# Short products ahead of the 256-column stages of a two-layer decoder trunk, and a low half that is issued later

## The chip, the cores and the metric

One core of one Trainium2 chip runs the whole kernel in one launch. The metric is device microseconds of one execution, the median of several runs. TensorE (PE), VectorE (DVE), ScalarE (ACT), GpSimd (POOL) and SyncE (SP) run at the same time, each with its own list of instructions in fixed order, and wait for each other by semaphores. A TensorE product shows in the trace as a weight load (PEld) and a matmul (PE).

## The reference

Two layers over a float32 input of 512 tokens by 1024 features. Each layer is a half-step SwiGLU feed-forward block (FFN), a mixer and a second half-step FFN:

```python
D_MODEL, SEQ, DEPTH, D_FF = 1024, 512, 2, 2816
def swiglu(h, w_gate, w_up, w_down):
    return (jax.nn.silu(h @ w_gate) * (h @ w_up)) @ w_down
# in each layer:
#   x += 1/2 * post(SwiGLU_1(pre(x)))
#   h = pre(x); P = h @ W_in    (HGRN2 q/f/i/out-gate, attention q/k/v, two branch gates)
#   A = HGRN2 recurrence(P) -> W_bA;  B = sliding-window attention(P) -> W_bB
#   x += post((sigmoid(gA)*A + sigmoid(gB)*B) @ W_out)
#   x += 1/2 * post(SwiGLU_2(pre(x)))
```

`pre` and `post` are RMS norms. The weights come from HBM once, as float32.

## The kernel before, in words

**Products.** TensorE works on a format that keeps part of a float32 number, so each float32 operand is split into a high half (`whi` for weights, the first `s` for activations) and a low half (`wlo`, the other `s`). One product is three matmuls, high by high, high by low and low by high (`mm3`, `wmm`). The weights lie in the array (128 rows by 128 columns) and the activations stream past, 512 tokens or a half of them, 256, at a time. All matmuls go through the helper `mm`, line L115. The order of TensorE's instructions is that in which the program's coroutines issue them; those of other engines are placed by a scheduler, except for instructions that are pinned in program order (`pin`, `hold` with `tight`).

**The weight stream.** `Stream` (`ws`) hands TensorE its weights in order, as items. Raw weights are loaded by SP into four buffers (`w32`, 128 by 1024 float32); an item's halves go into one of six pairs of tiles `whi` and `wlo`, 1024 columns in a tile of 1088, at the item's column offset `it.at`. `plain` makes items with offset 0, `pairs` makes four items a, b, c, d from two raw buffers with offset `ASIDE` = 16. Item a is the first raw buffer, b and c are sums of pieces of both (DVE, L339, L340, L346, L347), d is the last 512 columns of the second. `split` makes the halves: the high half is an ACT copy (L353). For b and c the low half is a DVE subtraction (L362). For a and d ("v" items too) ACT writes the weights with their sign turned into `wlo`, where they are cut like the high half (L357), and a DMA that POOL issues (L360) adds the raw weights to them; the low half is there when that DMA has landed. After d the two raw buffers are let go, and SP's next loads into them are issued.

**Stages.** In each FFN, `quad` comes first: four accumulators, over the first 256 tokens and then over the last 256, each half 8 steps `k` of 4 products of 256 columns (192 matmuls in both halves of a quad that has halves). There are five such quads, one in each mixer and in three of the FFNs; the first FFN has a quad without halves. The quads use the first four plain items. After some products of 512 columns come the rows of groups of seven (`fast`, `sevenths`): a row makes its gate and up products by seven products of half size in the place of eight, and takes 84 matmuls of 256 columns: 12 each for p1 and the first half of p26 (item a), 24 for both halves of p57 (item b), 24 for the second half of p26 and the first of p43 (item c), and 12 for the second half of p43 (item d). DVE puts the seven products together (L1054, L1056, L1060, L1061). The FFN of layer 0 that comes first has 15 rows, the others 19; each mixer has four such rows in its branches, each between other work. After the rows of an FFN comes `down`, with products of 512 columns, whose weights are made by DVE sums (L263), ACT (L287) and DVE (L295).

Of the kernel before, what the change touches and what calls it, by code (L numbers as in the profile page):

```python
# [7 lines left out]
F32 = mybir.dt.float32  # L8
# [3 lines left out]
ALU = mybir.AluOpType  # L12
# [3 lines left out]
P = 128  # L16
# [16 lines left out]
    first=0.0, spread=2300.0, squares=1700.0, lay=34500.0, laid=770.0, normed=7600.0, final=2600.0,  # L33
# [3 lines left out]
W32, WS, AHEAD, TAIL, FIRST, EARLY, LATE = 4, 6, 3, 4, 7, 4, 8  # L37
TURN = 0
SEVEN = 16
ASIDE = 16  # L40
ORDER = ("p1", "p3", "p7", "p2", "p6", "p5")
HEADS = (0, 4, 1, 5, 2, 6, 3, 7)

# [2 lines left out]
def trunk(ctx: ExitStack, tc: tile.TileContext, xin, wall, gains, lbT, hgain, sinks, c_dist, c_mask, c_ident, out):  # L46
    nc = tc.nc
# [99 lines left out]
    pin = tc.keep_in_program_order  # L147
# [10 lines left out]
    class Stream:  # L158
        def __init__(self):
            self.n, self.wall = 0, 0  # L160
            self.items = []
            self.raw, self.dma = {}, 0
            self.done, self.flight = 0, 0
            self.cur, self.c = 0, 0
            self.src = {}
            self.pinned = False
            self.most = AHEAD
            self.tight, self.gate = False, None
            self.side, self.freed = [], 0
            self.part = {}  # L170

        def plain(self, n, kind="u"):
            self.items += [Item(kind, self.n + i) for i in range(n)]
            for i in range(n):
                self.src.setdefault(self.n + i, self.wall + i)
            self.n += n
            self.wall += n
# [145 lines left out]
        def split(self):  # L323
            it = self.items[self.done]
            if it.kind[0] == "p":
                return self.quarter(it)
            u, last = it.u, it.kind in "uvd"
            self.load(u + (1 if it.kind in "uv" else 2))
            it.hi, it.lo = (sb.tile([P, D + 64], F32R, tag=t, name=nm(t), bufs=WS)[:, it.at : it.at + D] for t in ("whi", "wlo"))
            w, h = self.raw[u], (slice(0, D // 2), slice(D // 2, D))  # L330
            cols = (slice(0, D),)
            if it.kind == "u" and u < 2:
                cols = h
            if it.kind in "bcd":
                v = self.raw[u + 1]
            if it.kind == "b":

                self.t13 = sb.tile([P, D], F32, tag="tt", name=nm("tt"), bufs=2)
                pin(nc.vector.tensor_tensor(self.t13[:, h[0]], w[:, h[0]], v[:, h[0]], op=ALU.add))  # L339
                pin(nc.vector.tensor_tensor(self.t13[:, h[1]], v[:, h[0]], v[:, h[1]], op=ALU.add))  # L340
                w = self.t13
                self.product()
            elif it.kind == "c":

                t = sb.tile([P, D], F32, tag="tt", name=nm("tt"), bufs=2)
                pin(nc.vector.tensor_tensor(t[:, h[0]], self.t13[:, h[0]], v[:, h[1]], op=ALU.add))  # L346
                pin(nc.vector.tensor_tensor(t[:, h[1]], t[:, h[0]], w[:, h[1]], op=ALU.add))  # L347
                w = t
            elif it.kind == "d":
                w = v  # L350
                cols = h[1:]
            for c in cols:
                i = nc.scalar.copy(it.hi[:, c], w[:, c])  # L353
                if u < 6 or self.pinned or self.tight:
                    pin(i)
                if it.kind in "vad":
                    i = nc.scalar.mul(it.lo[:, c], w[:, c], -1.0)  # L357
                    if self.pinned or self.tight:
                        pin(i)
                    nc.gpsimd.dma_start(it.lo[:, c].bitcast(F32), w[:, c], accum_op=ALU.add)  # L360
                else:
                    self.hold(nc.vector.tensor_tensor(it.lo[:, c], w[:, c], it.hi[:, c].bitcast(F32), op=ALU.subtract))  # L362
            self.done += 1
            self.flight += 1
            if last:
                nu = u + (1 if it.kind in "uv" else 2)
                for i in range(u, nu):
                    self.raw.pop(i)
                    self.freed += 1
                self.load(self.freed + W32)  # L370

        def ahead(self):
            while self.done < min(len(self.items), self.cur + 1 + self.most) and self.flight < WS:
                self.split()

        def need(self, i):
            self.ahead()
            while self.done <= i:
                assert self.flight < WS
                self.split()  # L380
            return self.items[i]
# [27 lines left out]
    ws = Stream()  # L409
# [7 lines left out]
    def wmm(o, b, mv, start, stop, poll=True):  # L417

        mm3(o, b[2:], mv, start, stop)
        ws.used(b)  # L420
        if poll:
            order.poll()

    def cut(pair, c):
        return pair[0][:, c], pair[1][:, c]
# [568 lines left out]
    def quad(pre, halves):  # L994

        o = [acc() for _ in range(4)]
        blocks = {}
        ws.pinned = halves
        for half in (0, 1) if halves else (None,):
            c = WHOLE if half is None else HALF[half]  # L1000
            for k in range(KT):
                order.until(lambda: pre.have[half or 0] > k)
                for j in range(4):
                    if (k, j) not in blocks:
                        blocks[k, j] = ws.next(uses=2 if halves else 1)
                    wmm(o[j][:, c], blocks[k, j], cut(pre.h[k], c), k == 0, k == KT - 1)
            ws.pinned = False
        return o
# [17 lines left out]

    H2 = S // 2

    def sevenths(pre, between=lambda: None):

        def product(o, it, c, n):
            x = pre.operand(n)
            for k in range(4):
                wmm(o, ws.block(it, c + k), x[k], k == 0, k == 3)

        p1, p26, p57, p43 = acc()[:, :H2], acc(), acc(), aux()
        s, v = big()[:, :H2], big(F32, [P, 2, H2])
        w = ws.whole()  # L1040
        product(p1, w, 0, 1)
        ws.hold(nc.scalar.copy(s, p1))
        product(p26[:, :H2], w, 4, 2)
        between()
        w = ws.whole()
        product(p57[:, :H2], w, 0, 5)
        product(p57[:, H2:], w, 4, 7)
        c = ws.whole()
        product(p26[:, H2:], c, 0, 6)
        ws.product()  # L1050
        m = sb.tile([P, 4, H2], F32, tag="m", name=nm("m"), bufs=1)
        pairs = [p.rearrange("p (i t) -> p i t", i=2) for p in (p26, p57, p43)]

        ws.hold(nc.vector.tensor_tensor(m[:, 0:4:2, :], pairs[0], s.unsqueeze(1).to_broadcast([P, 2, H2]), op=ALU.add))  # L1054

        ws.hold(nc.vector.tensor_tensor(v, pairs[1], m[:, 2:3, :].to_broadcast([P, 2, H2]), op=ALU.add))  # L1056
        product(p43[:, :H2], c, 4, 4)
        product(p43[:, H2:], ws.whole(), 4, 3)

        ws.hold(nc.vector.tensor_tensor(m[:, 3, :], p57[:, :H2], v[:, 1, :], op=ALU.add))  # L1060
        ws.hold(nc.vector.tensor_tensor(m[:, 1:3, :], pairs[2], v[:, ::-1, :], op=ALU.add))  # L1061
        return m

    def fast(pre, a, start):
        def early():
            if j == FT - 1:
                for i in range(SEVEN, SEVEN + EARLY):
                    ws.part[i] = split(a[i])

        ws.tight = True  # L1070
        for j in range(start, FT):
            ws.most = AHEAD + (j < FT - 1)
            m = sevenths(pre, early)
            z = big(F32, [P, 2, H2])
            ws.hold(nc.scalar.activation(out=m[:, 0:2, :], in_=m[:, 0:2, :], func=AF.Silu))

            def gate(m=m, z=z):
                ws.hold(nc.vector.scalar_tensor_tensor(z, m[:, 0:2, :], -1.0, m[:, 2:4, :], op0=ALU.mult, op1=ALU.mult))

            ws.gate = gate  # L1080
            if j == FT - 1:
                ws.product()
            a.append(z.rearrange("p i t -> p (i t)"))
        ws.tight = False
# [389 lines left out]
    for l in range(DEPTH):  # L1474
        for n in (0, 2, 4):
            if n == 2:
                ws.plain(4, "v")
                ws.plain(2 * H + 2 + 8 + LATE * 3 // 2)
                for _ in range(KT - LATE // 2):
                    ws.gates()  # L1480
                ws.rows(KT, False)
            else:
                p = FIRST if l + n == 0 else 3
                ws.plain(4, "v" if l and not n else "u")
                ws.plain(min(2 * p, 8) - 4)
                ws.plain(max(2 * p - 8, 0), "v")
                ws.pairs(FT - p)
                ws.rows(FT, True)
# [154 lines left out]
```

## Time and profile before

| | |
|---|---|
| runs | 2056.76, 2056.75, 2055.87 us, median 2056.75 us |
| profiled execution | 2057.03 us, its span 2055.3 us |
| granted TensorE clock | 1.00 throughout |
| TensorE busy | 2044.0 us, 99% of the span, 13531 matmuls |
| VectorE busy | 1624.1 us, 79% |
| ScalarE busy | 1250.1 us, 61% |
| GpSimd busy | 267.6 us, 13% |
| HBM | 213.43 MB read, 14.73 MB written |

Where things are in the span: rows of the first FFN of layer 0 from 89 to 237 us, rows of its second FFN from 729 to 915 us, those of layer 1 from 1064 to 1249 us and from 1745 to 1933 us; each is followed by its `down`. The quads of the mixers and FFNs lie ahead of these stages (the first mixer's at about 349 to 372 us, the second FFN's at about 700 to 723 us). How to read the profile: busy time is the time in which an instruction of the engine was under way, and matmuls overlap, so that the share of TensorE is 99% at any distance between matmuls. The distance itself, from one matmul's start to the next one's, is read from the number of matmuls in a stretch (the xcount behind the busy time of a window, which counts also the two or three that are under way at its edge).

### The profile page before, as it was taken

The numbers are of one execution on the slowest core, as the hardware profiler recorded it, in microseconds if no ns is written. First come the engines' busy times: TensorE is split into PE (matmuls) and PEld (weight loads), VectorE is DVE, ScalarE is ACT, GpSimd is POOL, SyncE is SP. The second block draws the span as 40 slices with busy tenths as digits, with TensorE's granted clock in tenths as the row PEclk, the third lists the DMA queues.
The fourth block names the chain that finished last, engine by engine and source line by source line (L and its number), as shares of the span: only waits on it lengthen the run. The fifth ranks groups of instructions, "written<-read, shape, count | busy, mean of one in ns | idle before, by whom it ended". The sixth has DMA issues, their size and how long they took to land. (4 is left out here: it accounts for less than half of the span.)

```text
span 2055.3 us, 36503 instructions
## 1 busy us (share of the span) xinstructions
PE 2044.0 (99%) x13531; PEld 1831.3 (89%) x13531; DVE 1624.1 (79%) x2894; ACT 1250.1 (61%) x2213; POOL 267.6 (13%) x318
## 2 busy tenths in 40 slices
PE   9999999999999999999999999999999999999998
PEld 7899988877888999997899998888778989999987
DVE  5887889767676778888988788977686858788888
ACT  7556687446355556658866566864554545665684
POOL 0111140000000012113201111400000100111140
PEclk9999999999999999999999999999999999999999
DMA  8587798312247367879857778872122563788794
GB/s 256 148 188 191 175 206 239 114 64 70 73 101 207 113 151 189 189 187 208 206 151 189 192 187 207 177 232 85 62 73 62 140 193 99 181 189 195 176 199 123
DMA packets 166802, 328.07 MB, mean 160 GB/s; under 512 B 19072, under 2 KB 85088, under 8 KB 166624
## 3 DMA queue, kind: packets, MB, share of 16 engines
q1 hardware_dynamic: 122416, 228.16, 33.3%
q0 software_dynamic: 44064, 97.54, 28.2%
q8 instruction: 106, 1.74, 0.4%
q14 instruction: 72, 0.59, 0.1%
q10 hardware_dynamic: 144, 0.05, 0.0%
HBM read 213.43 MB, written 14.73 MB: 111 GB/s over the span
## 5 line engine op out<-in xcount | busy, mean ns | idle before, releaser
L115 PE MATMUL acc<-s,whi 128*128 128x256 f32 (+1 forms) x4976 | 1035.9, 306 | 0.4 <-ACT whi L353 0.4
L115 PEld LDWEIGHTS acc<-s,whi 128*128 128x128 f32 x4976 | 799.7, 189 | 47.2 <-issue 3.2
L115 PE MATMUL acc<-s,wlo 128*128 128x256 f32 (+1 forms) x2488 | 760.5, 306 | 1.0 <-DMA wlo<-w 0.8
L115 PEld LDWEIGHTS acc<-s,wlo 128*128 128x128 f32 x2488 | 468.9, 188 | 25.1 <-DMA wlo<-w 1.5
L115 PE MATMUL acc<-whi,s 128*128 128x512 f32 x1360 | 442.0, 393 | 1.4 <-DVE s L432 1.3
L353 ACT CAST whi<-w 128x1024 fp32r<-128x1024 f32 (+1 forms) x310 | 286.4, 928 | 151.0 <-PE acc L115 102.9
L353 ACT CAST whi<-tt 128x1024 fp32r<-128x1024 f32 x160 | 167.9, 1049 | 250.7 <-DVE tt L347 177.8
L360 POOL DMA_DIRECT2D wlo<-w x178 | 154.0, 867 | 1237.3 <-ACT wlo L357 532.0
L115 PEld LDWEIGHTS acc<-whi,s 128*128 128x128 f32 x1360 | 255.2, 188 | 59.6 <-issue 3.2
L362 DVE TENSOR_TENSOR wlo<-tt,whi 128x1024 fp32r<-128x1024 f32 x160 | 196.0, 1225 | 131.6 <-ACT whi L353 124.6
L115 PE MATMUL acc<-wlo,s 128*128 128x512 f32 x680 | 266.3, 392 | 1.2 <-DVE wlo L295 1.2
L115 PE MATMUL aux<-s,whi 128*128 128x256 f32 (+1 forms) x1296 | 233.1, 281 | 0.0
L362 DVE TENSOR_TENSOR wlo<-w,whi 128x1024 fp32r<-128x1024 f32 (+1 forms) x132 | 157.6, 1207 | 75.6 <-ACT whi L353 74.6
L115 PEld LDWEIGHTS aux<-s,whi 128*128 128x128 f32 x1296 | 199.1, 189 | 1.1 <-issue 0.5
L115 PE MATMUL aux<-s,wlo 128*128 128x256 f32 (+1 forms) x648 | 182.2, 281 | 0.0
L115 PEld LDWEIGHTS acc<-wlo,s 128*128 128x128 f32 x680 | 127.7, 188 | 30.0 <-DVE wlo L295 5.2
L357 ACT ACTIVATE wlo<-w 128x1024 fp32r<-128x1024 f32 (+1 forms) x178 | 153.7, 863 | 0.0
L115 PE MATMUL aux<-whi,s 128*128 128x512 f32 x432 | 143.8, 390 | 0.0
L443 POOL DMA_DIRECT2D s<-s x128 | 111.0, 969 | 218.4 <-ACT s L431 98.6
L115 PEld LDWEIGHTS aux<-s,wlo 128*128 128x128 f32 x648 | 121.9, 188 | 0.3
L295 DVE TENSOR_TENSOR wlo<-s,whi 128x512 fp32r<-128x512 f32 x160 | 103.0, 690 | 9.9 <-ACT whi L287 8.1
L431 ACT CAST s<-s 128x512 fp32r<-128x512 f32 (+1 forms) x140 | 70.8, 548 | 44.8 <-DVE s L490 39.3
(184 smaller groups left out, 2468.8 us busy)
## 6 DMA issues: line engine op xcount, KB each, us to landing
w<-wall SPq DMA_DIRECT2D x267, 512.0 KB, 4.2
wlo<-w POOLq DMA_DIRECT2D x98, 512.0 KB, 5.2
w<-wall SPq DMA_DIRECT2D x224, 128.0 KB, 3.6
wlo<-w POOLq DMA_DIRECT2D x80, 256.0 KB, 3.2
s<-wall SPq DMA_DIRECT2D x128, 128.0 KB, 4.1
s<-s POOLq DMA_DIRECT2D x64, 256.0 KB, 4.6
x_d<-s SPq DMA_DIRECT2D x48, 256.0 KB, 4.2
s<-x_d SPq DMA_DIRECT2D x48, 256.0 KB, 5.2
```

The costliest lines, as they stand in the source:

```text
L115: nc.tensor.matmul(o, lhsT, rhs, start=start, stop=stop)
L295: pin(nc.vector.tensor_tensor(it.lo[:, h[c]], w[c], it.hi[:, h[c]].bitcast(F32), op=ALU.subtract))
L353: i = nc.scalar.copy(it.hi[:, c], w[:, c])
L357: i = nc.scalar.mul(it.lo[:, c], w[:, c], -1.0)
L360: nc.gpsimd.dma_start(it.lo[:, c].bitcast(F32), w[:, c], accum_op=ALU.add)
L362: self.hold(nc.vector.tensor_tensor(it.lo[:, c], w[:, c], it.hi[:, c].bitcast(F32), op=ALU.subtract))
L431: (hold or ws.hold)(nc.scalar.copy(hi, src))
L443: nc.gpsimd.dma_start(lo.bitcast(F32), src, accum_op=ALU.add)
```

## The change

Three things are changed.

1. `lead` issues one matmul with `start` and `stop` whose result nobody reads; the next product starts its accumulator anew in the same place and overwrites it. It has 144 columns ahead of the first product of a run of rows: once ahead of each FFN's rows, and ahead of each of the 8 rows of the mixers, 12 in all. It has 112 columns ahead of the third of the 32 products of each half of each quad (step 0, accumulator 2), 10 in all. It has the same weights as the product behind it.
2. The four first items of every quad with halves get the column offset 16 in place of 0.
3. In the rows of the FFNs the low half of d is held back until the next item, which is the next row's a, is made: ACT does a high, a low and then d low, and POOL issues the DMA of a ahead of that of d. The two raw buffers of the pair are let go after d's low half, and the loads into them are issued from there. A d that is followed by another item than a is handled as before, and so are the mixers'.

```diff
+LEAD, LEAD_IN = 144, 112
...
-        def plain(self, n, kind="u"):
-            self.items += [Item(kind, self.n + i) for i in range(n)]
+        def plain(self, n, kind="u", at=0):
+            self.items += [Item(kind, self.n + i, at=at) for i in range(n)]
...
                 if it.kind in "vad":
-                    i = nc.scalar.mul(it.lo[:, c], w[:, c], -1.0)
-                    if self.pinned or self.tight:
-                        pin(i)
-                    nc.gpsimd.dma_start(it.lo[:, c].bitcast(F32), w[:, c], accum_op=ALU.add)
+                    def low(it=it, w=w, c=c):
+                        i = nc.scalar.mul(it.lo[:, c], w[:, c], -1.0)
+                        if self.pinned or self.tight:
+                            pin(i)
+                        nc.gpsimd.dma_start(it.lo[:, c].bitcast(F32), w[:, c], accum_op=ALU.add)
+                    nxt = self.items[self.done + 1].kind
+                    if it.kind == "d" and nxt == "a":
+                        self.low = low, self.done, u
+                    else:
+                        low()
+                        self.flush()
...
-            if last:
-                nu = u + (1 if it.kind in "uv" else 2)
-                for i in range(u, nu):
-                    self.raw.pop(i)
-                    self.freed += 1
-                self.load(self.freed + W32)
+            if last and not self.low:
+                self.free(u, u + (1 if it.kind in "uv" else 2))
...
+        def flush(self):
+            if self.low:
+                (low, _, u), self.low = self.low, None
+                low()
+                self.free(u, u + 2)
...
         def need(self, i):
             self.ahead()
+            if self.low and i >= self.low[1]:
+                self.flush()
...
+                    if halves and (k, j) == (0, 2):
+                        lead(o[j][:, c], blocks[k, j][2], pre.h[k][0][:, c], LEAD_IN)
                     wmm(o[j][:, c], blocks[k, j], cut(pre.h[k], c), k == 0, k == KT - 1)
...
+    def lead(o, st, mv, n):
+        mm(o[:, :n], st, mv[:, :n], True, True)
...
+        if first:
+            lead(p1, w.hi[:, :P], pre.operand(1)[0][0], LEAD)
         product(p1, w, 0, 1)
...
-            m = sevenths(pre, early)
+            m = sevenths(pre, early, j == start)
...
-                ws.plain(4, "v")
+                ws.plain(4, "v", ASIDE)
...
-                ws.plain(4, "v" if l and not n else "u")
+                ws.plain(4, "v" if l and not n else "u", ASIDE if l + n else 0)
```

On ACT, at the first rows of layer 0's first FFN, the halves of a d (the tile of 512 columns) and of the next row's a stood like this before:

```order
L353 CAST whi_983<-w_139_708 128x512
L357 ACTIVATE wlo_984<-w_139_708 128x512
L353 CAST whi_1019<-w_175_847 128x1024
L357 ACTIVATE wlo_1020<-w_175_847 128x1024
L1075 ACTIVATE m_1001<-m_1001 128x512
L353 CAST whi_1046<-tt_1048 128x1024
```

The same place of the changed kernel (a number behind a name is that of the buffer's use, and the code's lines are moved by some):

```order
L355 CAST whi_984<-w_139_708 128x512
L355 CAST whi_1014<-w_177_876 128x1024
L361 ACTIVATE wlo_1015<-w_177_876 128x1024
L361 ACTIVATE wlo_985<-w_139_708 128x512
L1104 ACTIVATE m_996<-m_996 128x512
L355 CAST whi_1047<-tt_1049 128x1024
```

The low half of d has moved behind both halves of a, and nothing else has moved between them; POOL's list shows the same exchange, the DMA of a's 1024 columns now ahead of that of d's 512.

On PE, where the first run of rows begins behind products of 512 columns, before:

```order
L115 MATMUL acc_880<-s_200,whi_703 128x512
L115 MATMUL acc_880<-s_199,wlo_704 128x512
L115 MATMUL acc_918<-s_598,whi_766 128x256 x2
L115 MATMUL acc_918<-s_598,wlo_767 128x256
L115 MATMUL acc_918<-s_623,whi_766 128x256 x2
```

And in the changed kernel:

```order
L116 MATMUL acc_880<-s_200,whi_703 128x512
L116 MATMUL acc_880<-s_199,wlo_704 128x512
L116 MATMUL acc_918<-s_598,whi_766 128x144
L116 MATMUL acc_918<-s_598,whi_766 128x256 x2
L116 MATMUL acc_918<-s_598,wlo_767 128x256
L116 MATMUL acc_918<-s_623,whi_766 128x256 x2
```

One matmul of 144 columns has come in; all of the others stand in the order of before. In the quads it is the same with 112 columns, here in the first mixer's:

```order
L116 MATMUL acc_4134<-s_4030,whi_3919 128x256
L116 MATMUL acc_4134<-s_4031,whi_3919 128x256
L116 MATMUL acc_4134<-s_4030,wlo_3920 128x256
L116 MATMUL acc_4135<-s_4030,whi_3919 128x256
L116 MATMUL acc_4135<-s_4031,whi_3919 128x256
L116 MATMUL acc_4135<-s_4030,wlo_3920 128x256
L116 MATMUL acc_4136<-s_4030,whi_3919 128x112
L116 MATMUL acc_4136<-s_4030,whi_3919 128x256
L116 MATMUL acc_4136<-s_4031,whi_3919 128x256
L116 MATMUL acc_4136<-s_4030,wlo_3920 128x256
```

Before, the same rows stand there without the one of 112 columns.

More of the change, by code (lines that the diff above doesn't have):

```diff
@@ L169, in __init__ @@
             self.side, self.freed = [], 0
+            self.low = None
             self.part = {}
-        def plain(self, n, kind="u"):
-            self.items += [Item(kind, self.n + i) for i in range(n)]
+        def plain(self, n, kind="u", at=0):
+            self.items += [Item(kind, self.n + i, at=at) for i in range(n)]
             for i in range(n):
@@ L364, in split, with free @@
             self.flight += 1
-            if last:
-                nu = u + (1 if it.kind in "uv" else 2)
-                for i in range(u, nu):
-                    self.raw.pop(i)
-                    self.freed += 1
-                self.load(self.freed + W32)
+            if last and not self.low:
+                self.free(u, u + (1 if it.kind in "uv" else 2))
+        def free(self, u, nu):
+            for i in range(u, nu):
+                self.raw.pop(i)
+                self.freed += 1
+            self.load(self.freed + W32)
         def ahead(self):
@@ L1027, in trunk, with sevenths @@
     H2 = S // 2
-    def sevenths(pre, between=lambda: None):
+    def lead(o, st, mv, n):
+        mm(o[:, :n], st, mv[:, :n], True, True)
+    def sevenths(pre, between=lambda: None, first=True):
         def product(o, it, c, n):
```

## The prediction

> **What bounds the kernel now.** I read the page first, then the number of matmuls in stretches of each stage, then the stretch around a short wait of a weight load, and last VectorE's loop and the waits of weight loads.
>
> ```profile
> PE 2044.0 (99%) x13531; PEld 1831.3 (89%) x13531; DVE 1624.1 (79%) x2894; ACT 1250.1 (61%) x2213; POOL 267.6 (13%) x318
> ```
>
> TensorE is busy for 99%, so time goes only where its matmuls come closer together, or fewer of them come. How close they come is in these windows, PE alone, matmuls in brackets: one of a quad, then rows of the FFNs in the order of the program.
>
> ```profile
> 360.00:372.00 12.00, 12.00 (x102) 1.00 0.46 168
> 90.00:140.00 50.00, 50.00 (x427) 1.00 0.79 188
> 790.00:845.00 55.00, 55.00 (x488) 1.00 0.81 191
> 1066.00:1120.00 54.00, 54.00 (x461) 1.00 0.76 180
> 1125.00:1199.00 74.00, 74.00 (x655) 1.00 0.81 192
> 1775.00:1919.00 144.00, 144.00 (x1225) 1.00 0.79 189
> ```
>
> All are matmuls of 256 columns at a granted clock of 1.00. Some 2.4 of each count are under way at the edges (0.28 us long, one each 0.118 us). Without them the step from one start to the next is 0.120 us in the quad (12.00 / 99.6), 0.118 in three of the rows' windows (50.00 / 424.6, 54.00 / 458.6, 144.00 / 1222.6), and 0.113 in the other two (55.00 / 485.6, 74.00 / 652.6). The fourth and fifth window are of one run of rows, which goes from 0.118 to 0.113 between them. This is the place:
>
> ```profile
> 1122.73 0.28 PE L115 MATMUL aux<-s,wlo 128*128 128x256 f32 x1
> 1123.08 0.28 PE L115 MATMUL aux<-s,wlo 128*128 128x256 f32 x1
> 1123.77 0.38 PE L115 MATMUL acc<-s,wlo 128*128 128x256 f32 x1 [0.17 <-DMA wlo<-w]
> 1124.57 0.28 PE L115 MATMUL acc<-s,wlo 128*128 128x256 f32 x1
> 1124.91 0.28 PE L115 MATMUL acc<-s,wlo 128*128 128x256 f32 x1
> ```
>
> Three matmuls take 0.35 us before the wait for a late low half (of the new row's a) and 0.34 after it, and that stays so for the whole next window. So the step is a state that a chain of matmuls keeps until something upsets how weight loads fall between matmuls. The quads' weights alone lie at offset 0, and theirs is the slowest step.
>
> A second chain stands beside it: VectorE, in two windows of 144 us within rows, and the first sum of two rows that follow each other.
>
> ```profile
> 1083.00:1227.00 144.00, 116.07 (x164) 1.00 0.79 191
> 1775.00:1919.00 144.00, 116.71 (x164) 1.00 0.79 189
> 1107.48 0.68 DVE L339 TENSOR_TENSOR tt<-w,w 128x512 f32<-128x512 f32 x1
> 1117.18 0.68 DVE L339 TENSOR_TENSOR tt<-w,w 128x512 f32<-128x512 f32 x1
> ```
>
> It issues 164 instructions in each, whatever TensorE's step; one row takes it 9.70 us (1117.18 - 1107.48). The 84 matmuls of a row take TensorE 9.89 us at 0.1178 and 9.52 at 0.1133: at the slow step VectorE's loop has room, at the quick one it is the longer of the two.
>
> **The change part by part.** Sums go against the profiled execution, 2057.03 us, which lies 0.28 over the median of the runs shown.
>
> *The quads.* Their weights get the rows' offset, and each half a matmul of another length. If both bring the quick step, a quad gains 192 x (0.1200 - 0.1133) = 1.29 us; with the rows' slow step 192 x 0.0022 = 0.42; else nothing. No matmul of 112 or 144 columns is in the trace. The nearest are transposes of 128 columns:
>
> ```profile
> 356.50:357.90 1.40, 1.40 (x15) 1.00 1.02 253
> ```
>
> That is 0.111 us each (1.40 / 12.6); 256 columns take 0.118, and the lower bound is nothing, where a lead only fills time in which the next weight load is under way. I take 0.115, between the rows, so two leads cost a quad 0.23. The mixers' two quads lie on TensorE's path: 2 x (1.29 - 0.23) = 2.1 us. In the FFNs' three another chain runs beside:
>
> ```profile
> 712.40 1.29 DVE L432 TENSOR_TENSOR s<-s,s 128x512 fp32r<-128x512 f32 x2 [1.39 <-ACT s L431]
> ```
>
> VectorE makes the quad's input there and waited 1.39 us for ACT, which gets no shorter by a closer step. I let 0.8 of the 1.29 pass (bounds 0 and 1.29): 3 x (0.8 - 0.23) = 1.7 us.
>
> *The mixers' rows.* Each of the eight is a chain of its own of 84 matmuls; a stretch of one:
>
> ```profile
> 619.00:627.00 8.00, 8.00 (x70) 1.00 0.88 207
> ```
>
> 8.00 / 67.6 is 0.118, the slow step. At the quick one a row gains 84 x 0.0045 = 0.38, less its lead 0.26. I count seven, since one of the eight has the quick step already, and the lead of that one: 7 x 0.26 - 0.115 = 1.7 us. If the leads do nothing, 8 x 0.115 = 0.9 us are lost.
>
> *The FFNs' rows.* At the quick step from the first row on, the first run's 15 rows and the last one's 19 would give TensorE 5.7 and 7.2 us, and the two runs between, quick in about half of their rows, 3 to 4 each. But VectorE's list goes from the last row straight on into the down stage. So I compare the end of a quick run with that of a slow one: the last row's first sum on VectorE, the last matmul of the rows, and a low half in the down stage.
>
> ```profile
> 1241.26 0.69 DVE L1054 TENSOR_TENSOR m<-acc,s 128x512 f32<-128x512 f32 x1
> 1248.90 0.28 PE L115 MATMUL aux<-s,wlo 128*128 128x256 f32 x1
> 1280.40 0.69 DVE L295 TENSOR_TENSOR wlo<-s,whi 128x512 fp32r<-128x512 f32 x1 [1.77 <-ACT whi L287]
> 1922.56 0.68 DVE L1054 TENSOR_TENSOR m<-acc,s 128x512 f32<-128x512 f32 x1
> 1933.30 0.28 PE L115 MATMUL aux<-s,wlo 128*128 128x256 f32 x1
> 1961.71 0.69 DVE L295 TENSOR_TENSOR wlo<-s,whi 128x512 fp32r<-128x512 f32 x1 [1.77 <-ACT whi L287]
> ```
>
> VectorE needs 39.14 and 39.15 us for the same way. TensorE ended 7.64 us behind the sum in the quick run and 10.74 in the slow one: against VectorE the quick step moved it up by 3.1 us. The down stage took that back. These are the waits of weight loads in the 67 us behind the quick run (behind the slow one none stand in as many):
>
> ```profile
> PEld acc L115 <- DVE s L432: 1.1, 1, 1.1
> PEld acc L115 <- DVE wlo L295: 0.9, 2, 0.6
> PEld aux L115 <- DVE wlo L295: 0.6, 1, 0.6
> PEld acc L115 <- ACT whi L287: 0.6, 1, 0.6
> PEld aux L115 <- ACT whi L287: 0.2, 1, 0.2
> ```
>
> Their sum is 3.4. So I count nothing for the two runs that are quick in part, and for the first and the last 0.8 each, leads taken off, of 0 to 3.1: a quarter, as a slow run's down stage shows no wait and so has some room. That is 1.6 us.
>
> *The low half of d.* One row before: the high half of c, d's low half, a's two halves, POOL's two DMAs, and how long those take to land.
>
> ```profile
> 1122.28 1.05 ACT L353 CAST whi<-tt 128x1024 fp32r<-128x1024 f32 x1 [2.40 <-DVE tt L347]
> 1123.75 0.63 ACT L357 ACTIVATE wlo<-w 128x512 fp32r<-128x512 f32 x1
> 1124.28 1.03 ACT L353 CAST whi<-w 128x1024 fp32r<-128x1024 f32 x1
> 1124.67 0.86 POOL L360 DMA_DIRECT2D wlo<-w  x1 [6.27 <-DVE wlo L362]
> 1125.22 1.06 ACT L357 ACTIVATE wlo<-w 128x1024 fp32r<-128x1024 f32 x1
> 1126.57 0.86 POOL L360 DMA_DIRECT2D wlo<-w  x1 [1.05 <-DVE m L1060]
> wlo<-w POOLq DMA_DIRECT2D x98, 512.0 KB, 5.2
> wlo<-w POOLq DMA_DIRECT2D x80, 256.0 KB, 3.2
> s<-s POOLq DMA_DIRECT2D x64, 256.0 KB, 4.6
> ```
>
> C is the end of c's high half, 1123.33. Before, d's DMA starts at C + 1.3 and lands at C + 4.5; a's at C + 3.2 and C + 8.4. After, a's two ACT instructions move up by the 0.53 us that d's low half took (1124.28 - 1123.75), and a lands at C + 7.9. d's low half ends at about C + 3.3, POOL, 0.29 us behind ACT before, starts it at C + 3.6, and it lands at C + 6.8 with 3.2, or C + 8.2 with the 4.6 of transfers of that size issued one behind another. The row that began at 1123.08 needs d 72 matmuls on, at C + 7.9. So d's slack goes from 3.4 us to something from +1.1 to -0.3. A wait there counts once in a run, as the later needs move with it; where VectorE is the limit it hides. I take 0.2 for each of the three later runs, 0.6, of 0 to 1.8. The Trainium skill, DMA: Bandwidth & Descriptors, section Queues, rings and completion order, says that each DMA engine consumes a ring's descriptors in order; by that d would land hardly before a's C + 7.9, and each run would wait up to 0.3.
>
> *Sum*: 2057.03 - 2.1 - 1.7 - 1.7 - 1.6 + 0.6 = 2050.5; less 0.28 for the median, 2050.3.
>
> **The rivals.** *Quick to the end.* If the down stages do not take the quick rows back, the first and the last run gain the whole 3.1: 2 x 2.3 more, 2045.7. For it: those two down stages show no wait of their own. Against: 3.4 us of waits behind a quick run. Chance 0.13.
>
> *The leads do not set the step.* Then 22 leads cost 2.5 us, the quads gain 5 x 0.42 = 2.1 by their offset or nothing, and a, landing earlier, no longer waits and sets no quick state, which costs nothing, as it brought nothing. With 0.6 for d it is 2057.8 to 2059.9. For it: all runs of rows start at 0.118 behind products of 512 columns, though the length changes there too; against: a wait of 0.2 us sufficed. By the Trainium skill, TensorE: Matmul & The Clock Gate, section Step-by-step: what each phase is for, weight loads and the streamed operand have independent read ports, and loading the next weights takes nothing from the running matmul; then neither offset nor phase could matter and the time would be 2059.9. The steps of 0.113, 0.118 and 0.120 for one form of matmul do not agree with it. Chance 0.2.
>
> *The raw weights come late*, the slower side. A pair's raw buffers are let go when d's DMA has landed, at C + 6.8 to 8.2 in place of C + 4.5. The next load into them takes
>
> ```profile
> w<-wall SPq DMA_DIRECT2D x267, 512.0 KB, 4.2
> ```
>
> so it is there at C + 11.0 to 12.4, and later if two loads share the DMA engines. VectorE's L339 reads it two loops behind 1117.18, at C + 13.25. From a landing 0.8 us later than my later value, every row of VectorE's loop gets longer: 0.1 us in each of 72 rows make 7, 0.2 make 14, less the 5.5 of quads and mixers: 2058 to 2065. For it: DMA engines are 0.79 busy there; against: the 0.8 us left. Chance 0.25.
>
> **How the numbers follow.** The forecast has 0.42. A measurement of this kernel can tell about 0.2% from no change, 4.1 us: faster is under 2052.6, slower over 2060.9. Faster: 0.39 of the forecast's 0.42 (the rest has d's waits at their top or quads at 0.118), and the quick rival's 0.13, 0.52. Slower: 0.21 of the late raw weights' 0.25, and 0.04 of the idle leads' 0.2, with d's waits of 1.8: 0.25. The same: 0.23. The range reaches from 2043, the quick rival with leads that cost nothing (22 x 0.115 = 2.5), to 2062, the middle of the late weights; 0.1 lie above it and some 0.05 below.
>
> **What would show it.** Right: a quad's 102 matmuls in 12 us become 108; rows have some 444 in 50 us from the first row of every run; VectorE's 164 in 144 us stay; weight loads wait for L295 and L432 behind all four runs; d's DMA starts at C + 3.6. Wrong: rows that stay at 427 in 50 us (idle leads), a loop of VectorE over 9.8 us with L339 waiting for raw weights (late weights), or no waits behind quick rows (quick to the end).

## The result, and the profile after

The changed kernel takes 2061.68 us (median of 8 runs, 2059.24 to 2064.22), the kernel before 2056.05 us (8 runs, 2055.45 to 2056.76). The ratio is 1.0026, 95% interval 1.0017 to 1.0035: slower by 5.6 us, where 2050.3 was forecast. The profiled execution took 2063.16 us, its span 2061.4 us.

Behind the leads the matmuls come closer together, as forecast, but in the later runs of rows that does not last. The page's first line and the windows that the prediction showed, PE alone (quad, then rows of the FFNs), in the changed kernel:

```profile
PE 2040.8 (99%) x13553; PEld 1827.3 (89%) x13553; DVE 1625.5 (79%) x2894; ACT 1251.8 (61%) x2213; POOL 269.3 (13%) x318
360.00:372.00 12.00, 12.00 (x104) 1.00 0.41 145
90.00:140.00 50.00, 50.00 (x441) 1.00 0.72 187
790.00:845.00 55.00, 54.49 (x470) 1.00 0.75 195
1066.00:1120.00 54.00, 50.91 (x417) 0.94 0.65 162
1125.00:1199.00 74.00, 74.00 (x633) 1.00 0.74 184
1775.00:1919.00 144.00, 141.95 (x1214) 1.00 0.73 185
```

Behind the lead 441 matmuls stand in the first run's 50 us where 427 stood. In the three later runs fewer stand than before. One reason is the step, the distance from one matmul's start to the next one's: a wait can set it back to 0.118 us, and in the window from 790 us the kernel without the held-back half (the first experiment below) has 470 matmuls too, and no wait. The other is that three of these windows have time in which no matmul is under way. The waits say for what: first TensorE's weight loads for low halves that a DMA brings, then VectorE's first sum of a row (L341, formerly L339) for raw weights, in the changed kernel:

```profile
PEld aux L116 <- DMA wlo<-w: 14.5, 15, 3.3
PEld acc L116 <- DMA wlo<-w: 1.3, 1, 1.3
DVE tt L341 <- DMA w<-wall: 11.3, 13, 2.7
```

In the kernel before no weight load for `aux` waits for a DMA, and the other two rows are these:

```profile
PEld acc L115 <- DMA wlo<-w: 1.5, 3, 0.8
DVE tt L339 <- DMA w<-wall: 4.3, 2, 2.1
```

`aux` is the accumulator of the products that use the items c and d, and of these two only d has a low half that a DMA brings, so 14.5 us are waits for d's low half. Of L341's 13 waits two stand in the mixers, as before; eleven are new, in the rows of the FFNs, 6.3 us together. They lengthen VectorE's loop. Its first sum of the first and of the last row in the second FFN of layer 0, before (L339) and after:

```profile
733.47 0.68 DVE L339 TENSOR_TENSOR tt<-w,w 128x512 f32<-128x512 f32 x1
899.14 0.68 DVE L339 TENSOR_TENSOR tt<-w,w 128x512 f32<-128x512 f32 x1
733.02 0.69 DVE L341 TENSOR_TENSOR tt<-w,w 128x512 f32<-128x512 f32 x1
903.01 0.69 DVE L341 TENSOR_TENSOR tt<-w,w 128x512 f32<-128x512 f32 x1 [1.45 <-DMA w<-wall]
```

That is 165.67 us before and 169.99 after. The two FFNs of layer 1 have 165.94 and 165.63 before, 169.91 and 167.43 after: 10.1 us more in the three together. One row of the changed kernel, in the second FFN of layer 0, shows how the two hang together (ACT, POOL, VectorE, the weight load of d, SP):

```profile
778.32 1.05 ACT L355 CAST whi<-tt 128x1024 fp32r<-128x1024 f32 x1 [2.40 <-DVE tt L349]
780.75 1.57 ACT L361 ACTIVATE wlo<-w 128x1024 fp32r<-128x1024 f32 x2
782.10 1.75 POOL L364 DMA_DIRECT2D wlo<-w  x2 [7.97 <-ACT wlo L361]
782.68 1.17 POOL L364 DMA_DIRECT2D wlo<-w  x1
782.93 0.68 DVE L341 TENSOR_TENSOR tt<-w,w 128x512 f32<-128x512 f32 x1
789.55 0.19 PEld L116 LDWEIGHTS aux<-s,wlo 128*128 128x128 f32 x1 [1.10 <-DMA wlo<-w]
789.56 0.80 SPq L248 DMA_DIRECT2D w<-wall  x2
793.18 0.69 DVE L341 TENSOR_TENSOR tt<-w,w 128x512 f32<-128x512 f32 x1 [0.46 <-DMA w<-wall]
```

C, the end of c's high half, is 779.37. POOL issues a and d one behind the other from 782.10 on (the line of 782.68 shows the second of the two alone), and d has landed at 789.55, C + 10.2. In that moment TensorE goes on after 1.10 us, and SP, which had stood there, issues two loads in a row: the one into the buffer that d's DMA had read, and the next pair's first, which stood behind it in SP's queue. VectorE waits for the first of the two: 3.6 us later, at 793.18, it has the raw weights, 10.25 us after its sum of the row before; a loop without a wait takes 9.70. The page's transfers, issue to landing, after:

```profile
wlo<-w POOLq DMA_DIRECT2D x98, 512.0 KB, 4.8
wlo<-w POOLq DMA_DIRECT2D x80, 256.0 KB, 5.4
```

Those of d need 5.4 us where they needed 3.2, those of a 4.8 where they needed 5.2: d's transfer, half as large, now takes longer than a's. In all of the 68 rows that have the two DMAs one behind the other d lands behind a, by 1.3 us in the median.

### The profile page after: what moved, and what is told of

Read it like the earlier page. It is cut to its first block, busy times and chain, and to the rows that moved or that the text cites. A ratio compares the mean times of both kernels' runs of the same rounds, so it can differ in the third digit from the quotient of the medians.

```text
span 2061.4 us, 36438 instructions
## 1 busy us (share of the span) xinstructions
PE 2040.8 (99%) x13553; PEld 1827.3 (89%) x13553; DVE 1625.5 (79%) x2894; ACT 1251.8 (61%) x2213; POOL 269.3 (13%) x318
## 5 line engine op out<-in xcount | busy, mean ns | idle before, releaser
L361 ACT ACTIVATE wlo<-w 128x1024 fp32r<-128x1024 f32 (+1 forms) x178 | 146.2, 858 | 0.0
L116 PEld LDWEIGHTS aux<-s,wlo 128*128 128x128 f32 x648 | 122.6, 189 | 14.9 <-DMA wlo<-w 14.5
L297 DVE TENSOR_TENSOR wlo<-s,whi 128x512 fp32r<-128x512 f32 x160 | 102.7, 686 | 9.9 <-ACT whi L289 8.1
```

Source lines behind the costliest of these rows:

```text
L116: nc.tensor.matmul(o, lhsT, rhs, start=start, stop=stop)
L297: pin(nc.vector.tensor_tensor(it.lo[:, h[c]], w[c], it.hi[:, h[c]].bitcast(F32), op=ALU.subtract))
```

## The experiments

In what follows theory A is that d's low half lands late because its DMA stands behind that of a, and that this is the loss; theory B that the leads and the offset are, or that the quick step is given back whatever stands behind it.

**Without the held-back half.**

```diff
-                    if it.kind == "d" and nxt == "a":
+                    if False:
```

> All of the change but the held-back low half of d. Theory A (the held-back low half makes d land behind a, and its waits are the loss): the weight loads' waits for d (14.5 us in the changed kernel) go, a waits a little as in the quick rows before (up to 3 us); 2050 to 2053 us. Theory B (leads and offset are the loss, or the quick step is given back whatever stands behind it): 2056 to 2059 us. Both expect 0.113 us a matmul at the beginning of every run of rows.

2052.95 us, ratio to before 0.9983 (0.9974 to 0.9992): faster than before. Weight loads wait for a, and for d no more than once, 0.6 us; behind each of the four runs of rows the down stage waits once for VectorE (L453, formerly L432), as the prediction expected of quick rows:

```profile
PEld acc L116 <- DMA wlo<-w: 6.6, 11, 1.8
PEld acc L116 <- DVE wlo L297: 5.9, 14, 0.6
PEld acc L116 <- DVE s L453: 3.5, 4, 1.1
```

Theory B falls: the leads and the offset bring some 3.6 us. They do not shorten VectorE's loop: its first sums of the first and the last row of the three later runs are 165.70, 166.02 and 165.73 us apart, as before.

**Only the held-back half.** No leads, the quads at offset 0.

```diff
-                    if halves and (k, j) == (0, 2):
+                    if False:
...
-        if first:
+        if False:
...
-                ws.plain(4, "v", ASIDE)
+                ws.plain(4, "v")
...
```

> Of the change only the held-back low half of d; no lead, quads at offset 0. Theory A: rows run at 0.118 us a matmul and d's slack, 2 to 5 us before, falls by some 4 us; it waits in the early rows of the three later runs, 1 to 3 us each, 2058 to 2062 us. Theory B: no change, 2055.5 to 2057 us.

2064.09 us, ratio 1.0039 (1.0027 to 1.0052), 7.5 us slower than before and past the range expected. The waits are those of the whole change, without any lead:

```profile
PEld aux L116 <- DMA wlo<-w: 14.3, 15, 2.2
DVE tt L341 <- DMA w<-wall: 10.2, 15, 2.1
```

So the held-back half costs its 7 to 9 us without the leads as well. Some of its waits set the quick step here too, but others stand behind stretches at 0.118 us, so it is not only that quick rows ask for d sooner.

**Leads and offset in quads and mixers alone, and leads of the FFNs' rows alone.** Both are without the held-back half. The first leaves out the leads of the FFNs' rows, by the edit shown; the second leaves out the offset and all other leads.

```diff
-            m = sevenths(pre, early, j == start)
+            m = sevenths(pre, early, False)
```

> Offset 16 in the quads, their leads, and the leads of the mixers' eight rows; no leads ahead of the FFNs' rows, no held-back low half. Theory A: the quads start each run of rows some 0.3 us earlier as in the changed kernel, the mixers' rows give 1 to 2 us; 2052 to 2054.5 us. Theory B: 2055.5 to 2058 us.

> Only the four leads ahead of the FFNs' rows; quads at offset 0, no leads in quads and mixers, no held-back low half. Theory A: rows start at 0.113 us, a waits in the early rows, VectorE's loop stays at 9.70 us a row and the down stages wait for VectorE; 2053.5 to 2056.5 us. Theory B: 2056 to 2058 us.

2053.06 us (0.9983, 0.9974 to 0.9992) and 2055.37 us (0.9994, 0.9985 to 1.0003): the quads and the mixers bring 3.5 us, the FFNs' leads about 1.2, and that is not clear of no change. Both times lie in the ranges of theory A. They add up to 4.7, no different within these intervals from the 3.6 of both together.

**Only POOL's order.** ACT's list as before, POOL's DMA of d held behind that of a.

```diff
+                    i = nc.scalar.mul(it.lo[:, c], w[:, c], -1.0)
+                    if self.pinned or self.tight:
+                        pin(i)
+
                     def low(it=it, w=w, c=c):
-                        i = nc.scalar.mul(it.lo[:, c], w[:, c], -1.0)
-                        if self.pinned or self.tight:
+                        i = nc.gpsimd.dma_start(it.lo[:, c].bitcast(F32), w[:, c], accum_op=ALU.add)
+                        if self.tight and it.kind in "ad":
                             pin(i)
-                        nc.gpsimd.dma_start(it.lo[:, c].bitcast(F32), w[:, c], accum_op=ALU.add)
```

> The changed kernel with ACT's list as before (d low ahead of a's halves) and only POOL's DMA of d held behind that of a. Theory A1 (d's transfer is served behind a's, and that makes it late): as late as in the changed kernel or later, 2060 to 2065 us. Theory A2 (d is late because ACT makes its low half later): d's DMA starts earlier than in the changed kernel and its waits halve, 2054 to 2058 us.

2071.32 us, ratio 1.0075 (1.0062 to 1.0088), slower than the whole change by some 10 us though ACT has d's low half ready first, and above both of the ranges expected. Its waits, and d's transfer:

```profile
PEld aux L116 <- DMA wlo<-w: 30.5, 21, 3.8
DVE tt L341 <- DMA w<-wall: 20.4, 21, 2.8
wlo<-w POOLq DMA_DIRECT2D x80, 256.0 KB, 5.3
```

On ACT a follows d's low half again, so a is issued later than in the changed kernel, and d behind it: counted from C, d is issued at 3.8 us in the median and lands at 9.25, against 3.3 and 9.0 in the changed kernel. That the order of the two DMAs is what matters, and not ACT's, is shown by this run and the next. Why so small a shift costs 10 us more was not followed up.

**d between a's halves.** ACT: d high, a high, d low, a low; POOL's d ahead of a again.

```diff
                     else:
+                        self.flush()
                         low()
-                        self.flush()
```

> The changed kernel, but ACT makes d's low half between a's high and a's low half, so that POOL issues d ahead of a and a no earlier than before. Theory A1: d lands some 3.2 us after its issue, 1 us later than before, and does not wait; 2051.5 to 2054 us. Theory A2: a third to a half of the loss stays, 2055 to 2058 us.

2051.25 us, ratio 0.9979 (0.997 to 0.9988), just below theory A1's range. d starts later than in the kernel before (C + 2.3 in the median, not 1.35), but ahead of a. In this run's waits and transfers

```profile
wlo<-w POOLq DMA_DIRECT2D x80, 256.0 KB, 3.3
DVE tt L341 <- DMA w<-wall: 4.4, 2, 2.3
PEld acc L116 <- DMA wlo<-w: 5.6, 9, 1.1
```

it takes 3.3 us and no weight load waits for it; the two waits of L341 are those in the mixers. Against the run without any holding back, 2052.95, the intervals overlap.

**Five raw buffers.** The whole change, and for the control the kernel without the held-back half, with

```diff
-SLOTS = 61
+SLOTS = 59
...
-W32, WS, AHEAD, TAIL, FIRST, EARLY, LATE = 4, 6, 3, 4, 7, 4, 8
+W32, WS, AHEAD, TAIL, FIRST, EARLY, LATE = 5, 6, 3, 4, 7, 4, 8
```

> The changed kernel with five raw buffers in place of four (and 59 slots of working space in place of 61), so that the next raw weights do not wait for d's DMA. If the late raw weights (L341 waits 11.3 us in 13 places) carry the loss: those waits go, d's waits shrink with them, 2052 to 2056 us. If TensorE's own waits for d carry it: 14 us of waits stay, 2058 to 2063 us.

> The kernel without the held-back half (all leads and the offset) with five raw buffers and 59 slots: the control of the run before with five raw buffers. If a fifth buffer only takes away the waits that the held-back half made: as without it, 2052 to 2054 us. If it brings something of its own: 2048 to 2051 us, and holding d's half back costs a little even with five buffers.

2051.32 us (0.9978, 0.9969 to 0.9987; runs from 2049.08 to 2055.76) and 2048.04 us (0.996, 0.9946 to 0.9973). The first lies below both of the ranges expected, the control in that of a gain of its own. No wait of L341 for raw weights is left in either. In the first, d's waits add up to as much as ever:

```profile
PEld aux L116 <- DMA wlo<-w: 14.2, 22, 1.7
```

Without the control this run would have been misread: a fifth buffer brings 4.9 us of its own (2052.95 to 2048.04), about what the two waits of L341 in the mixers had (5.2 us in the kernel without the held-back half). Set against its control, the held-back half costs 3.3 us with five raw buffers; with four it costs 8.7 (2061.68 against 2052.95, from two sets of runs whose before differed by 0.5). So at least some 5.4 of its 8.7 us go through the raw weights, and VectorE's loop says more: its three later runs of rows are 9.9 us longer in the changed kernel than without the held-back half (in two profiles that lie 10.3 apart), and with five raw buffers 0.1 us longer than in the control. What is left there, 14.2 us of TensorE's waits, costs 3.3, so most of it lies beside VectorE's loop. In these two profiles, 2.7 us apart, TensorE's last products of d come 1.5 to 4.6 us later than in the control in the three later runs, and each down stage behind them takes 0.5 to 0.8 us longer.

**d's low half on POOL.** No held-back half, and for d in the FFNs' rows a subtraction on POOL in place of ACT's and the DMA.

```diff
+                        if it.kind == "d" and self.tight:
+                            nc.gpsimd.tensor_tensor(it.lo[:, c], w[:, c], it.hi[:, c].bitcast(F32), op=ALU.subtract)
+                            return
```

> All leads and the offset, no held-back half, and in the FFNs' rows d's low half made by a POOL subtraction in place of ACT and a DMA. a starts 0.6 us earlier with nothing ahead of it in the queue and lands in 4.5 us. If a's waits (6.6 us in e1) are worth their time: 2050 to 2052.5 us. If VectorE's loop is the limit all the same: 2052 to 2053.5 us. If POOL's subtraction slows VectorE's by 0.1 us or more a row: 2056 us and over.

2054.32 us, ratio 0.999 (0.9981 to 0.9999): no better than with the DMA. None of the three expectations met it. VectorE's loop was hardly slowed, 164 instructions in 144 us as before, but a's own transfer took longer, and it still waited:

```profile
wlo<-w POOLq DMA_DIRECT2D x98, 512.0 KB, 6.3
PEld acc L116 <- DMA wlo<-w: 4.0, 8, 0.8
756.00:900.00 144.00, 116.10 (x164) 1.00 0.63 162
```

Why a takes 6.3 us with less in its queue stays open.

**Other lengths of the lead.** No held-back half; ahead of the rows 240, 256, 192, 176, 160, 208, 128, 128, 112, 96, 64 and 32 columns, and in the second halves of the quads 144, 128, 176, 208 and 64.

> No held-back half; leads of other lengths: ahead of the twelve runs of rows 240, 256, 192, 176, 160, 208, 128, 128, 112, 96, 64 and 32 columns, and in the five quads 112 in the first half and 144, 128, 176, 208 and 64 in the second. If it is any upset of the chain that sets the step: all rows but those behind 256 start at 0.113 us. If it is the length of the lead against the next weight load: only lengths near 144 do. In the quads' second halves, 0.118 behind 112, some other length gives 0.113. The time says nothing here, 2050 to 2058 us.

2052.54 us in a single run. Rows of the first mixer behind 256, 176 and 160 columns:

```profile
588.00:596.00 8.00, 8.00 (x71) 1.00 0.68 167
619.00:627.00 8.00, 8.00 (x73) 1.00 0.85 200
634.00:642.00 8.00, 8.00 (x73) 1.00 0.83 267
```

Only the lead of 256, as long as the products behind it, left the row at the slow step; behind all of the other lengths it is the quick one. Behind 192 columns that shows nothing of the lead, as a wait for a came two matmuls later. In the quads' second halves it was otherwise: behind 144 to 208 columns 0.118 stayed, and behind 64 it became 0.113. The first and the last quad's second half:

```profile
361.50:372.00 10.50, 10.50 (x91) 1.00 0.37 126
1720.50:1730.30 9.80, 9.80 (x89) 1.00 0.28 54
```

**Put together.** d between a's halves with five raw buffers, and the same with 64 columns in the quads' second halves:

```diff
-                        lead(o[j][:, c], blocks[k, j][2], pre.h[k][0][:, c], LEAD_IN)
+                        lead(o[j][:, c], blocks[k, j][2], pre.h[k][0][:, c], 64 if half else LEAD_IN)
```

> d's low half between a's two halves on ACT, and five raw buffers. If raw weights have room there already: as with four, 2050.5 to 2053 us. If the fifth buffer brings something of its own, 2046 to 2050 us.

> The kernel with d's low half between a's and five raw buffers, with 64 columns in place of 112 in the lead of the quads' second halves. In the run with other lengths the second half of a quad took 10.3 us behind 64 columns and 10.6 to 10.7 behind longer ones. If all five do so and TensorE is the limit there: 5 x 0.35 less, 2045.5 to 2047 us. If the FFNs' quads are held by VectorE: only the mixers' two count, 2046.5 to 2047.5 us.

2047.39 us (0.9957, 0.9944 to 0.9969) and 2046.84 us (0.9953, 0.994 to 0.9967). The second half of the first mixer's quad, in the former and then in the latter:

```profile
360.00:370.00 10.00, 10.00 (x87) 1.00 0.43 149
360.00:370.00 10.00, 10.00 (x90) 1.00 0.37 120
```

The last step is 0.55 us, less than the intervals can tell, and lies in both of the ranges expected; the whole is about 9.6 us faster than the kernel before, and 15 faster than the changed one.

## Why the prediction was wrong

**The step that failed** is "The low half of d". Its issue at C + 3.6 was nearly right (the second of the two DMAs starts at 782.68, C + 3.3, C being 779.37; 3.3 is the median too). Its landing, "C + 6.8 with 3.2, or C + 8.2 with the 4.6", was not: 4.6 us came from transfers of 256 KB behind others of their own size, and d now stands behind one twice as large. It took 5.4 in the median and landed at C + 9.0 in the median of 68 rows, in all but one between C + 8.5 and C + 12.0, and at C + 10.2 in the row shown. The sentence on ring order in the Trainium skill, DMA: Bandwidth & Descriptors, section Queues, rings and completion order, spoke for the later end, and the trace agrees with it: d landed behind a in all 68 rows. The prediction took that order only for a wait of up to 0.3 us, since it gave d the moment at which a lands, C + 7.9 (7.45 in the median), and no time after it, where 1.3 us passed. The term was 0.6 us and measured 7.5 alone and 8.7 in the whole change.

The moment at which d is needed was read too early, which made the slack too small and not too large. The prediction counts 72 matmuls from 1123.08 to C + 7.9, but leaves out that row's wait for a, and d's low half is used first by the third matmul of d. The weight load in the kernel before:

```profile
1131.94 0.19 PEld L115 LDWEIGHTS aux<-s,wlo 128*128 128x128 f32 x1
```

That is C + 8.6, C being 1123.33 there.

**The rival "The raw weights come late"** had named the mechanism, its place and the point from which it decides, a landing 0.8 us past C + 8.2. C + 10.2 is past it, and so are half of the landings. Its chance of 0.25 was too low for a reason within reach: the 0.8 us of room were counted from C + 8.2, and that figure came from transfers behind others of their own size. Its size was right, 7 to 14 us for the rows: VectorE's three later runs of rows got 10.1 us longer, of which L341's eleven waits are 6.3, and the other parts of the change gave some of it back. The rival did not think of SP's queue, in which a load that waits for d holds the next pair's first load behind it. That this cost anything is not shown: in the row above that second load landed at 794.35, and VectorE reads it only in the next row, some 9.7 us behind 793.18.

**"Where VectorE is the limit it hides"** was right for TensorE's own waits, most of them: with five raw buffers 14.2 us of them cost 3.3.

**The quads** were sized too high. The first halves have the quick step (the first mixer's, before and after, in the first two lines below), the second ones 0.118, so that 102 matmuls in 12 us became 104 and not 108. With the mixers' rows they bring 3.5 us where 5.5 were forecast (2.1, 1.7 and 1.7). The mixers' rows took the quick step (the third line; it had 70 before), with one of them held 1.3 us by a late a (the `acc` row of the waits above). What the offset does without a lead was not tried.

```profile
349.00:356.00 7.00, 7.00 (x61) 1.00 1.05 284
349.00:356.00 7.00, 7.00 (x64) 1.00 1.00 285
619.00:627.00 8.00, 8.00 (x73) 1.00 0.86 205
```

**The FFNs' leads** were forecast at 1.6 and measured at 1.2, not clear of nothing. Closer matmuls were given back to VectorE's loop as worked out, with the waits for L297 and L453 behind the runs. But the forecast of 5.7 and 7.2 us for TensorE took a run that starts quick to stay quick to its end, and in the kernel without the held-back half only the first run did so; the last section shows what ended it in another.

**The idle leads** did not come. From the section of the Trainium skill, TensorE: Matmul & The Clock Gate, that it named, the prediction had worked out that neither offset nor phase would matter; the steps of 0.113, 0.118 and 0.120, now set by a lead's length where a chain begins, speak against that once more. The prediction's own reason, that a wait upsets how weight loads fall between matmuls, is not shown: at both steps a weight load starts within 0.01 us of a matmul's start.

## What to carry to other kernels

A transfer that is moved behind another in one queue landed behind that other one here, every time, so its landing is worked out from the other one's and not from its own time alone, and then followed to everything that its landing lets go: here not only the product that reads the tile, but the source buffer, the load into it, and the loop that reads that load two rounds on. A wait that looks harmless because another engine is the limit is to be checked against that engine's own inputs. And an experiment that adds a buffer needs the control that adds it alone: of the 10.4 us that it seemed to show here (2061.68 to 2051.32), 4.9 were the buffer's own gain elsewhere.

## What the runs showed of the hardware

Ahead of a run of rows, a throw-away matmul of any tried length from 32 to 240 columns (192 apart, where a wait hid it) set the step of the 256-column matmuls behind it at 0.113 us, and one of 256 columns left it at 0.118. In the quads' second halves only 64 columns did so. That is a gain of 4% in TensorE's rate for one short instruction, but it lasts only until the next wait or change of stage, and a wait can set either step. In the kernel without the held-back half, in the second FFN of layer 0, a wait of 0.19 us ended the quick step:

```profile
776.50:786.50 10.00, 10.00 (x90) 1.00 0.78 195
786.70 0.19 PEld L116 LDWEIGHTS acc<-s,wlo 128*128 128x128 f32 x1 [0.19 <-DMA wlo<-w]
787.00:797.00 10.00, 10.00 (x87) 1.00 0.79 195
```

From there to the end of the rows, 128 us, it stayed at 0.118; before the change a wait in the same run had brought the quick step. What decides which of the two a wait leaves is open.

A single long wait can cost more than its time. In the changed kernel's third run of rows, TensorE stood still for more than 3 us for d's low half, and the granted clock (the column behind the matmuls) fell to half for the next microseconds:

```profile
1085.80:1089.00 3.20, 0.34 (x1) 0.83 0.32 59
1089.00:1091.00 2.00, 2.00 (x11) 0.50 0.62 170
1091.00:1093.00 2.00, 2.00 (x11) 0.50 1.07 393
1093.00:1097.00 4.00, 4.00 (x30) 0.78 0.93 177
```

11 matmuls in 2 us stand where some 18 would. The first line's mean of 0.83 over 3.2 us makes 1.1 us at half the clock, so it fell at about 1087.9, some 2.3 us behind the end of the last matmul, 1085.6. The Trainium skill, TensorE: Matmul & The Clock Gate, section Part 1: The HAM clock gate (the "warmup" mystery), gives an idle window of about 3.4 us behind which the clock is halved, in a window that runs free. The halving is as it says, but here it came before the engine had been idle for so long. The run with POOL's order alone, with a wait of 3.8 us and a granted clock of 1.00 throughout, shows that not every long wait meets it. The changed kernel's runs had a mean clock from 0.998 to 1.0 and lie 5 us apart, those of the kernel before 1.3; that the clock makes that spread was not tried.
